# Gate and branch projections with 512 moving columns, a reordered beginning and a new weave in a hybrid decoder block

## The chip, the core and the metric

The kernel runs on one core of a Trainium2 chip. The metric is the device time of one execution in microseconds, lower is better; the time before is the median of three runs, 1659.07 us (1658.06 to 1659.58). TensorE (PE) multiplies, VectorE (DVE), ScalarE (ACT) and GpSimd (POOL) do the elementwise work, and SyncE (SP) issues most of the loads. PE takes a stationary operand of up to 128x128 (a weight load, PEld) and streams the columns of a moving operand past it into PSUM.

## What is computed

One layer (DEPTH is 1) of a decoder trunk over 256 tokens and 2048 channels in float32. Cut to what matters:

```python
mod = silu(c) @ w_ada + b_ada            # six vectors of 2048: sh1 sc1 g1 sh2 sc2 g2
h = rms_norm(x, mix_norm_pre) * (1 + sc1) + sh1
a_q, a_f, a_i, a_g, b_q, b_k, b_v, c_a, c_g = split(h @ w_in)
ya = hgrn2_mixer(a_q, a_f, a_i, a_g, ...)      # gated linear recurrence, 8 heads
yb = dilated_attention_mixer(b_q, b_k, b_v, rel_bias)
yc = conv_module(c_a, c_g, ...)                # 31-tap depthwise convolution, layer norm, swish
gates = sigmoid(h @ w_gate + b_gate)           # three gates of 2048 columns
merged = g0 * (ya @ w_a_out) + g1 * (yb @ w_b_out) + g2 * (yc @ w_c_out)
x = x + g1 * rms_norm(merged @ w_o, mix_norm_post)
h = rms_norm(x, mlp_norm_pre) * (1 + sc2) + sh2
x = x + g2 * rms_norm(square(relu(h @ w_up)) @ w_down, mlp_norm_post)
```

## The kernel before

All products of activations and weights are made in three passes of a reduced float type (fp32r). A weight tile of 128x1024 float32 (512 KB) is loaded into one of six `raw` buffers; ACT casts it into `hi` (line 126), DVE subtracts to get `lo` (line 127), six buffers each; PE then adds hi x hi, hi x lo and lo x hi. The work is a list of some 540 such **jobs**, run in order by `run`: it issues loads up to five jobs ahead and splits up to four jobs ahead, then emits the matmuls of job i, and then `work(budget)` lets generators emit a little side work: `chain` holds attention, the recurrence (`hgrn_prep`, `hgrn_levels`, `hgrn_out`) and small row builders, `filler` holds the convolution (`conv_gen`, 31 taps on DVE, line 452) and its layer norm. A scheduler then fixes the order on every engine, so each engine's queue is in order.

There are two ways to multiply. `mm_a` (lines 242 to 254) keeps 128 output channels on the PSUM partitions: the weight tile is stationary and the 256 tokens move, 24 matmuls of 256 columns in a job. `mm_b` (lines 256 to 266) keeps 128 tokens on the partitions: the activations are stationary and 512 weight columns move, 12 matmuls of 512 columns in a job.

```python
nc.tensor.matmul(o, h[:, i, w], x, start=f and b0, stop=False, skip_group_check=True)   # mm_a
nc.tensor.matmul(o, ah[i][:, tk], h[:, i, :], start=f, stop=False)                      # mm_b
```

The order of the jobs is: eight chunks of `wada0` (the modulation of the first 256 channels, made on PE by `ada_pe_jobs`); the 13 units of the input projection in four strips of the contraction (`start_job`, ten units by `mm_a`, three by `mm_b`); 20 `v_job`s (`mm_b`); 96 `gate_job`s and 32 `proj_job`s (`mm_a`); 32 `o_job`s (`mm_b`); up-projection; down-projection. Between them stand 184 `ada` jobs, which load 512 KB and make a weighted sum over it on DVE (line 297). `weave` spreads the last 128 of these (g1 and m2 before, g2 in the up-projection) over the main jobs by weights; before, the first 32 gate jobs (W0) have none.

A gate is finished by four ACT sigmoids of 256 columns with the bias as a per-partition scalar (line 840). A branch is finished by a product (line 900) and a sum (line 904) on DVE, the third branch also by a hi/lo split (lines 908, 909). Between the last `o_job` and the up-projection, per half of the tokens, stand a norm (`post_o`, `norm_x2`, `make_h2`) and the splits of the first up-projection tiles; four of these lo parts are made on POOL (`UPOOL`).

Of the kernel before, what the change touches and what calls it, by code (L numbers as in the profile page):

```python
# [56 lines left out]
def hybrid_block(ctx: ExitStack, tc: tile.TileContext, a, out, dbg=None):  # L57
# [216 lines left out]
    nc.vector.tensor_mul(cact, cact, V("c"))  # L274
    cbc = []

    def bcast_cols(ps, cols, n):

        for j in range(n):
            nc.tensor.matmul(ps[:, j * P:(j + 1) * P], cols[:, j:j + 1].to_broadcast([P, P]), ident, start=True, stop=True)  # L280

    def make_cbc():
        for q in range(2):
            cbc.append(s4([P, 1024]))
            ps = ps_unit().rearrange("p a b -> p (a b)")
            bcast_cols(ps, cact[:, 8 * q:8 * q + 8], 8)
            nc.scalar.copy(cbc[q], ps)
# [19 lines left out]
    def ada_pe_jobs(finish):  # L307

        st = {}

        def fn(raw, ch):
            if ch == 0:
                st["ps"] = bank()
            for i in range(2):
# [2 lines left out]
                nc.tensor.matmul(st["ps"][32 * g:32 * g + 32, :], cact[:, kt:kt + 1].to_broadcast([P, 32]), raw[:, i, :],
                                 start=kt < 4, stop=kt >= 12, skip_group_check=True)
            if ch == 3:
                make_cbc()  # L320
            if ch == 7:
                acc = s2([P, 512])
                nc.scalar.mul(acc, st["ps"], 1.0 / 32)
                ps = bank()
# [971 lines left out]
```

## Time and profile before

| | |
|---|---|
| median of three runs | 1659.07 us (1658.06 to 1659.58) |
| the profiled execution, its own time | 1659.91 us |
| its span, first to last instruction | 1658.1 us |
| PE busy | 1622.5 us (98% of the span) |
| DVE busy | 1201.3 us (72%) |
| ACT busy | 735.4 us (44%) |
| POOL busy | 47.2 us (3%) |
| DMA moved | 403.21 MB, mean 243 GB/s |

Busy time of PE is modelled: matmuls overlap, so the mean duration of one (284 ns for 256 columns) is more than the distance between two. The rate is read from how many matmuls stand in a window that PE fills. For the other engines the distance of two starts is a little less than a duration.

### The profile page before, as it was taken

What the parts mean: (1) busy time and instruction counts of PE and PEld (TensorE: products, weight loads), DVE (VectorE), ACT (ScalarE), POOL (GpSimd) and SP (SyncE); (2) the same over time, 40 slices, a digit from 0 to 9 for tenths busy, and PEclk for the clock granted to TensorE, in tenths of its full rate; (3) what the DMA queues carried; (4) which work ended last, traced back from release to release, by engine and by line L of the source; (5) the groups of instructions that cost most, each with busy time, mean ns of one, the idle gap of its engine ahead of it and who ended that gap; (6) DMA issues with size and microseconds to landing.
All of it is one profiled execution on the core that took longest, in us unless ns stands there. A gap on an engine that the chain in (4) does not pass through costs nothing.

```text
span 1658.1 us, 25901 instructions
## 1 busy us (share of the span) xinstructions
PE 1622.5 (98%) x10198; PEld 1453.8 (88%) x10198; DVE 1201.3 (72%) x1625; ACT 735.4 (44%) x899; POOL 47.2 (3%) x74
## 2 busy tenths in 40 slices
PE   5999999999999999999999899999999999999997
PEld 3899999978999999999988788888888888888886
DVE  6799989868798998887897766666566845444444
ACT  3644444354443454434444554444434644333333
POOL 1000002000000000000000300000000000000000
PEclk9999999999999999999999999999999999999999
DMA  8999997645353899899988467777777676666662
GB/s 300 324 328 336 325 334 252 180 144 166 98 158 95 281 320 369 333 350 328 315 323 305 157 228 243 235 243 244 241 249 245 208 222 206 193 191 197 193 192 77
DMA packets 112106, 403.21 MB, mean 243 GB/s; under 512 B 13124, under 2 KB 13552, under 8 KB 111984
## 3 DMA queue, kind: packets, MB, share of 16 engines
q1 hardware_dynamic: 107280, 388.24, 69.5%
q0 software_dynamic: 4416, 13.18, 2.7%
q8 instruction: 80, 1.31, 0.3%
q14 instruction: 42, 0.34, 0.1%
q10 hardware_dynamic: 288, 0.13, 0.0%
HBM read 397.28 MB, written 6.59 MB: 244 GB/s over the span
## 4 chain that ended last, share of the span: by engine, by line
PE 93%; DVE 3%; ACT 2%; DMA 1%; issue 1%; POOL 0%; DVEq 0%; SPq 0%; ACTq 0%; POOLq 0%
PE g L1093 14%; PE g L254 11%; PE g L252 11%; PE g L253 11%; PE g L1095 7%; PE g L1170 5%; PE g L1171 5%; PE g L1172 5%; PE g L266 4%; PE g L265 4%; PE g L264 4%; PE m L1170 2%; PE m L1171 2%; PE m L1172 2%; PE m L566 2%; DVE lo L127 1%
## 5 line engine op out<-in xcount | busy, mean ns | idle before, releaser
L126 ACT CAST hi<-raw 128x1024 fp32r<-128x1024 f32 x538 | 563.9, 1052 | 787.2 <-PE g L1093 190.0
L127 DVE TENSOR_TENSOR lo<-raw,hi 128x1024 fp32r<-128x1024 f32 x534 | 646.4, 1220 | 256.6 <-ACT hi L126 255.0
L254 PE MATMUL g<-s,lo 128*128 128x256 f32 x1600 | 455.3, 285 | 1.2 <-DVE lo L127 1.2
L252 PE MATMUL g<-s,hi 128*128 128x256 f32 x1600 | 454.9, 284 | 0.0
L253 PE MATMUL g<-s,hi 128*128 128x256 f32 x1600 | 454.1, 284 | 0.0
L1093 PE MATMUL g<-s,hi 128*128 128x512 f32 x960 | 336.5, 397 | 0.0
L254 PEld LDWEIGHTS g<-s,lo 128*128 128x128 f32 x1600 | 307.3, 192 | 2.8 <-DVE lo L127 2.1
L252 PEld LDWEIGHTS g<-s,hi 128*128 128x128 f32 x1600 | 307.4, 192 | 1.6 <-issue 1.5
L253 PEld LDWEIGHTS g<-s,hi 128*128 128x128 f32 x1600 | 307.4, 192 | 0.4 <-issue 0.3
L297 DVE SCALAR_TENSOR_TENSOR raw<-raw,s 128x1024 f32<-128x1024 f32 x184 | 223.9, 1218 | 112.9 <-DMA raw<-wada 112.9
L1095 PE MATMUL g<-s,lo 128*128 128x256 f32 x960 | 268.0, 279 | 0.0
L1093 PEld LDWEIGHTS g<-s,hi 128*128 128x128 f32 x960 | 180.4, 188 | 43.9 <-issue 0.9
L1095 PEld LDWEIGHTS g<-s,lo 128*128 128x128 f32 x960 | 181.0, 188 | 0.0
L1172 PE MATMUL g<-hi,s 128*128 128x512 f32 x384 | 149.6, 389 | 0.0
L1170 PE MATMUL g<-hi,s 128*128 128x512 f32 x384 | 149.5, 389 | 0.0
L1171 PE MATMUL g<-lo,s 128*128 128x512 f32 x384 | 149.5, 389 | 0.0
L266 PE MATMUL g<-hi,s 128*128 128x512 f32 (+1 forms) x344 | 132.7, 386 | 2.9 <-DVE s L971 2.3
L264 PE MATMUL g<-hi,s 128*128 128x512 f32 (+1 forms) x344 | 132.2, 384 | 0.0
L265 PE MATMUL g<-lo,s 128*128 128x512 f32 (+1 forms) x344 | 131.8, 383 | 0.3 <-DVE lo L127 0.3
L1172 PEld LDWEIGHTS g<-hi,s 128*128 128x128 f32 x384 | 72.1, 188 | 15.0
L1170 PEld LDWEIGHTS g<-hi,s 128*128 128x128 f32 x384 | 72.1, 188 | 15.0
L1171 PEld LDWEIGHTS g<-lo,s 128*128 128x128 f32 x384 | 72.1, 188 | 14.8
(223 smaller groups left out, 1369.7 us busy)
## 6 DMA issues: line engine op xcount, KB each, us to landing
raw<-wada SPq DMA_DIRECT2D x192, 512.0 KB, 5.2
raw<-wu SPq DMA_DIRECT2D x128, 512.0 KB, 4.6
raw<-wd SPq DMA_DIRECT2D x128, 512.0 KB, 4.3
raw<-wg SPq DMA_DIRECT2D x96, 512.0 KB, 4.8
raw<-w SPq DMA_DIRECT2D x80, 512.0 KB, 5.2
raw<-wv SPq DMA_DIRECT2D x44, 512.0 KB, 3.9
raw<-wp SPq DMA_DIRECT2D x32, 512.0 KB, 5.8
raw<-wo SPq DMA_DIRECT2D x32, 512.0 KB, 5.2
```

The costliest lines, as they stand in the source:

```text
L126: nc.scalar.copy(h, raw)
L127: (eng or nc.vector).tensor_sub(l, raw, h.bitcast(F32))
L252: nc.tensor.matmul(o, h[:, i, w], x, start=f and b0, stop=False, skip_group_check=True)
L253: nc.tensor.matmul(o, h[:, i, w], y, start=False, stop=False, skip_group_check=True)
L254: nc.tensor.matmul(o, l[:, i, w], x, start=False, stop=e and b1, skip_group_check=True)
L266: nc.tensor.matmul(o, al[i][:, tk], h[:, i, :], start=False, stop=e)
L297: nc.vector.scalar_tensor_tensor(raw, raw, 1.0, cbc[q % 2], op0=ALU.mult, op1=ALU.mult, accum_out=st["p"][:, q:q + 1])
L1093: nc.tensor.matmul(ps[:, j, :], h[:, i, w], xy.rearrange("p a b -> p (a b)"), start=f, stop=False, skip_group_check=True)
L1095: nc.tensor.matmul(ps[:, j, 0:S], l[:, i, w], xy[:, 0, :], start=False, stop=e, skip_group_check=True)
L1170: nc.tensor.matmul(o, uh[:, kt % 4, tk], h[:, 0, w], start=kt == 0, stop=False)
L1171: nc.tensor.matmul(o, uh[:, kt % 4, tk], l[:, 0, w], start=False, stop=False)
L1172: nc.tensor.matmul(o, ul[:, kt % 4, tk], h[:, 0, w], start=False, stop=kt == 63)
```

## The change

It has six parts. (1) `gate_job` and `proj_job` use `mm_b`. The bias of a gate is now a row: POOL loads 512 columns of it into all partitions, DVE adds it out of PSUM, and one ACT sigmoid follows. The merged sum has tokens on partitions, so `merge_gen` turns it by 8 PE transposes for each n, with the hi/lo split in two halves. (2) The beginning is one function `begin`: `wada0` goes to eight buffers of its own, the token sums use adds instead of reductions, and `issue_after` ties fix the order on PE, ACT and DVE. (3) `ADA_AT` lets the first ada job come after three start jobs. (4) W0 goes from 32 to 8, and the weights of the weave change; 40 of the m2 jobs come before the g1 jobs. (5) BLS, the budget of the last input strip, goes from 0.4 to 0.8. (6) `UPOOL` is empty.

```diff
-BLS = 0.4
+BLS = 0.8
+ADA_AT = 3.0
-W0 = 32
-WG = 1.25
-WG2 = 1.25
+W0 = 8
+WG = 0.75
-WO = 1.2
+WO = 0.9
...
-            nc.vector.tensor_reduce(rd, sq.rearrange("p k s -> p s k"), axis=AX.X, op=ALU.add)
-            if q:
-                nc.vector.tensor_add(rd, rd, tot)
+            nc.vector.tensor_add(sq[:, 0:2, :], sq[:, 0:2, :], sq[:, 2:4, :])
+            if tot is not None:
+                nc.vector.tensor_add(sq[:, 0:2, :], sq[:, 0:2, :], tot[:, 0:2, :])
...
+        for ch in range(8):
+            t = s4([P, 2, 512])
+            nc.sync.dma_start(t, a["wada0"][ch].rearrange("p (a b) -> p a b", a=2))
+            raws.append(t)
...
     def gate_job(b, n, ch):
...
-            mm_a(pst["gt"], h, l, 2, [h_hi(k) for k in kts], [h_lo(k) for k in kts], ch == 0, ch == 7)
+            mm_b(pst["gt"], h, l, 2, [h_hi(k) for k in kts], [h_lo(k) for k in kts], ch == 0, ch == 7)
             if ch == 7:
-                gates[b, n] = s4([P, 4, S])
-                for j in range(4):
-                    c = b * 16 + n * 4 + j
-                    g = nc.scalar.activation(gates[b, n][:, j, :], pst["gt"][:, j // 2, (j % 2) * S:(j % 2 + 1) * S],
-                                             AF.Sigmoid, bias=V("bg")[:, c:c + 1])
+                g = gates[b, n] = s4([P, 2, 512])
+                nc.vector.tensor_add(g, pst["gt"], pst["gb"][:, None, :].to_broadcast([P, 2, 512]))
+                e = nc.scalar.activation(g, g, AF.Sigmoid)
...
+    def merge_gen(n):
...
+        for q in range(2):
+            ps = bank()
+            for j in range(2):
+                for t in range(2):
+                    nc.tensor.transpose(ps[:, j * S + t * P:j * S + (t + 1) * P],
+                                        merged[n][:, t, (2 * q + j) * P:(2 * q + j + 1) * P], ident)
+            psv = ps.rearrange("p (a b) -> p a b", a=2)
+            k = slice(2 * q, 2 * q + 2)
+            nc.scalar.copy(mh[:, k, :], psv)
+            nc.vector.tensor_sub(ml[:, k, :], psv, mh[:, k, :].bitcast(F32))
+            yield 0.6
...
-            mm_a(pst["pj"], h, l, 2, [t[:, 0, 0, :], t[:, 0, 1, :]], [t[:, 1, 0, :], t[:, 1, 1, :]], first, last)
+            mm_b(pst["pj"], h, l, 2, [t[:, 0, 0, :], t[:, 0, 1, :]], [t[:, 1, 0, :], t[:, 1, 1, :]], first, last)
...
-    UPOOL = (4, 5, 6, 7)
+    UPOOL = ()
...
-    jobs += weave([(gj[W0:72], WG), (pj[:8], WP), (gj[72:], WG2), (pj[8:], WP), (oj[:-10], WO)], g1_jobs + m2_jobs)
+    jobs += weave([(gj[W0:72], WG), (pj[:8], WP), (gj[72:], WG), (pj[8:], WP), (oj[:-10], WO)],
+                  m2_jobs[:40] + g1_jobs + m2_jobs[40:])
```

The order of the instructions that follows from it is shown at three places. **PE at the very beginning.** L317 before and L326 after is the modulation of the first channels from `wada0` (`raw` before, `s` after), L280 and L284 are broadcasts of `cact` and of the token norm `xr`, L363 and L384 the token sums. Before:

```order
L317 MATMUL m_166<-raw_154,cact 32x512
L363 MATMUL g_101<-ones,s_13_118 128x1 x2
L317 MATMUL m_166<-raw_154,cact 32x512
L317 MATMUL m_166<-raw_156,cact 32x512 x2
L280 MATMUL g_182<-ident,cact 128x128 x2
L317 MATMUL m_166<-raw_158,cact 32x512 x2
L280 MATMUL g_182<-ident,cact 128x128 x2
L280 MATMUL g_101<-ident,xr_123 128x128 x2
L317 MATMUL m_166<-raw_160,cact 32x512 x2
L280 MATMUL g_182<-ident,cact 128x128 x4
L280 MATMUL g_193<-ident,cact 128x128 x8
L317 MATMUL m_166<-raw_162,cact 32x512 x2
```

And after:

```order
L284 MATMUL g_118<-ident,cact 128x128 x8
L284 MATMUL g_127<-ident,cact 128x128 x8
L326 MATMUL m_117<-s_5_101,cact 32x512 x2
L326 MATMUL m_117<-s_6_103,cact 32x512 x2
L384 MATMUL g_136<-ones,s_20_148 128x1 x4
L326 MATMUL m_117<-s_7_105,cact 32x512 x2
L326 MATMUL m_117<-s_8_107,cact 32x512 x2
L326 MATMUL m_117<-s_9_109,cact 32x512 x2
L284 MATMUL g_136<-ident,xr_164 128x128 x2
L326 MATMUL m_117<-s_10_111,cact 32x512 x2
```

The 16 broadcasts of `cact` now stand ahead of everything, and the loads they used to separate are no longer in the `raw` ring.

**DVE in the first woven gate jobs.** The `hgrn_levels` of the first four heads make seven levels; in each, PE multiplies, DVE copies under a mask (COPY_PREDICATED) and makes two products. L127 and L128 are the lo parts of gate jobs, L452 and L488 convolution taps, L878 the new gate bias. Before, levels three and four:

```order
L569 COPY_PREDICATED s_657_4195<-masks,m_4401 128x128x4
L577 TENSOR_TENSOR s_647_4122<-s_647_4122,s_666_4273 128x128x4
L578 TENSOR_TENSOR s_648_4123<-s_648_4123,s_666_4273 128x128x4
L583 TENSOR_TENSOR s_666_4273<-s_666_4273 128x16
L452 SCALAR_TENSOR_TENSOR s_698_4581<-s_693_4537,vec,s_698_4581 128x256 x2
L127 TENSOR_TENSOR lo_4622<-raw_4584,hi_4621 128x1024
L569 COPY_PREDICATED s_657_4195<-masks,m_4446 128x64x8
L577 TENSOR_TENSOR s_647_4122<-s_647_4122,s_666_4273 128x64x8
L578 TENSOR_TENSOR s_648_4123<-s_648_4123,s_666_4273 128x64x8
L452 SCALAR_TENSOR_TENSOR s_698_4581<-s_693_4537,vec,s_698_4581 128x256 x2
L127 TENSOR_TENSOR lo_4671<-raw_4619,hi_4670 128x1024
```

And after, levels five and six:

```order
L878 TENSOR_TENSOR s_698_4549<-g_4343,s_673_4344 128x1024
L488 SCALAR_TENSOR_TENSOR s_687_4450<-s_683_4426,vec,s_687_4450 128x256
L605 COPY_PREDICATED s_653_4197<-masks,m_4471 128x32x16
L613 TENSOR_TENSOR s_643_4124<-s_643_4124,s_662_4275 128x32x16
L614 TENSOR_TENSOR s_644_4125<-s_644_4125,s_662_4275 128x32x16
L488 SCALAR_TENSOR_TENSOR s_687_4450<-s_683_4426,vec,s_687_4450 128x256 x3
L605 COPY_PREDICATED s_653_4197<-masks,m_4500 128x16x32
L613 TENSOR_TENSOR s_643_4124<-s_643_4124,s_662_4275 128x16x32
L614 TENSOR_TENSOR s_644_4125<-s_644_4125,s_662_4275 128x16x32
L488 SCALAR_TENSOR_TENSOR s_687_4450<-s_683_4426,vec,s_687_4450 128x256 x2
L128 TENSOR_TENSOR lo_4618<-raw_4611,hi_4617 128x1024
```

Before, a lo part stood behind nearly every level; after, 33 rows stand between two lo parts here (the last 10 of them are shown).

**DVE between the output and the up-projection**, behind the scale of the first token half (`diag`). L962 and L1015 make h2, L971 and L1024 its lo part. Before, the lo parts of four more tiles are on POOL:

```order
L947 TENSOR_SCALAR diag_151<-ident,r_150 128x128
L127 TENSOR_TENSOR lo_9815<-raw_9680,hi_9814 128x1024
L127 TENSOR_TENSOR lo_9864<-raw_9686,hi_9863 128x1024
L962 TENSOR_SCALAR s_1430_9803<-m_9798,mod_86 128x128
L962 TENSOR_SCALAR s_1436_9823<-m_9818,mod_86 128x128
```

And after:

```order
L1000 TENSOR_SCALAR diag_223<-ident,r_222 128x128
L128 TENSOR_TENSOR lo_8325<-raw_8190,hi_8324 128x1024
L128 TENSOR_TENSOR lo_8374<-raw_8196,hi_8373 128x1024
L1015 TENSOR_SCALAR s_1446_8313<-m_8308,mod_86 128x128
L128 TENSOR_TENSOR lo_8406<-raw_8198,hi_8405 128x1024
L1015 TENSOR_SCALAR s_1446_8313<-m_8308,mod_86 128x128
L1015 TENSOR_SCALAR s_1452_8333<-m_8328,mod_86 128x128
L1024 TENSOR_TENSOR s_1447_8318<-s_1446_8313,s_1447_8318 128x2x128
L128 TENSOR_TENSOR lo_8412<-raw_8409,hi_8411 128x1024
```

Six lo parts now stand on DVE up to the second `diag`, where two did.

## Rows read from the trace of the kernel before

**Rows 1.** The page, part 1 and the chain that ended last.

```profile
PE 1622.5 (98%) x10198; PEld 1453.8 (88%) x10198; DVE 1201.3 (72%) x1625; ACT 735.4 (44%) x899; POOL 47.2 (3%) x74
...
PE 93%; DVE 3%; ACT 2%; DMA 1%; issue 1%; POOL 0%; DVEq 0%; SPq 0%; ACTq 0%; POOLq 0%
```

**Rows 2.** Windows: a stage of gate jobs and a stage of `mm_b` jobs.

```profile
core 0: us, PE busy (x) PEld busy (x) DVE busy (x) ACT busy (x) POOL busy (x), PEclk, DMA share, GB/s
...
700.00:750.00 50.00, 50.00 (x419) 50.00 (x418) 41.71 (x59) 21.42 (x26) 0.00 (x0) 1.00 0.96 349
850.00:900.00 50.00, 50.00 (x222) 41.45 (x221) 40.41 (x54) 22.08 (x28) 0.00 (x0) 1.00 0.94 351
```

**Rows 3.** Timeline of the beginning: start us, us, engine, line, operation.

```profile
3.07 16.66 SPq L112 DMA_DIRECT2D raw<-wada  x8
...
10.26 1.06 ACT L356 ACTIVATE s<-s 128x1024 f32<-128x1024 f32 x1 [0.23 <-DMA s<-xT]
...
17.09 0.16 DVE L215 TENSOR_SCALAR rv<-g 128x2 f32<-128x2 f32 x1 [1.10 <-PE g L363]
...
19.27 0.16 DVE L222 SCALAR_TENSOR_TENSOR xr<-rt,ry 128x2 f32<-128x2 f32 x1
...
27.10 1.92 PE L317 MATMUL m<-raw,cact 128*32 128x512 f32 x16
...
33.03 0.58 PE L252 MATMUL m<-s,hi 128*128 128x256 f32 x1 [2.21 <-ACT hi L126]
```

**Rows 4.** Window of gate jobs 9 to 36, columns as in rows 2.

```profile
451.40:564.30 112.90, 111.34 (x942) 110.63 (x941) 103.31 (x191) 49.78 (x94) 0.00 (x0) 1.00 0.50 158
```

**Rows 5.** Groups by line: busy us, mean ns, idle before, releaser.

```profile
L900 DVE TENSOR_TENSOR s<-g,s 128x1024 f32<-128x1024 f32 x12 | 14.7, 1221 | 2.5 <-PE g L254 2.4
...
L721 PE MATMUL m<-ident,s 128*128 128x128 f32 x36 | 6.1, 279 | 0.0
```

**Rows 6.** The chain in order of time: 16 matmuls of 128 columns in a row.

```profile
949.73 1.80 PE m L954 x16
```

**Rows 7.** Windows of the beginning, columns as in rows 2.

```profile
10.00:15.00 5.00, 1.88 (x2) 0.18 (x2) 5.00 (x4) 1.09 (x2) 0.00 (x0) 1.00 1.03 419
15.00:20.00 5.00, 3.96 (x16) 2.06 (x16) 2.92 (x15) 0.00 (x0) 3.09 (x7) 1.00 0.57 193
```

**Rows 8.** Waits from 34 to 250 us: us in total, times, longest.

```profile
ACT hi L126 <- DMA raw<-w: 49.9, 33, 3.4
```

**Rows 9.** Timeline of DVE: two lo parts in a row.

```profile
907.09 1.22 DVE L127 TENSOR_TENSOR lo<-raw,hi 128x1024 fp32r<-128x1024 f32 x1
908.22 1.22 DVE L127 TENSOR_TENSOR s<-raw,s 128x1024 fp32r<-128x1024 f32 x1
```

**Rows 10.** Groups by line in the window of rows 4, columns as in rows 5.

```profile
L127 DVE TENSOR_TENSOR lo<-raw,hi 128x1024 fp32r<-128x1024 f32 x29 | 35.3, 1217 | 1.2 <-ACT hi L126 1.2
L452 DVE SCALAR_TENSOR_TENSOR s<-s,vec,s 128x256 f32<-128x256 f32 x60 | 26.5, 477 | 0.0
L569 DVE COPY_PREDICATED s<-masks,m 128x512 f32<-128x512 uint8 x11 | 9.2, 837 | 8.2 <-PE m L566 8.2
L297 DVE SCALAR_TENSOR_TENSOR raw<-raw,s 128x1024 f32<-128x1024 f32 x7 | 8.5, 1213 | 0.0
L578 DVE TENSOR_TENSOR s<-s,s 128x512 f32<-128x512 f32 x12 | 8.2, 682 | 0.0
```

**Rows 11.** Timeline of POOL between output and up-projection.

```profile
925.76 7.70 POOL L127 TENSOR_TENSOR lo<-raw,hi 128x1024 fp32r<-128x1024 f32 x3 [106.15 <-ACT hi L126]
```

**Rows 12.** Timeline of DVE in the same place.

```profile
923.47 0.29 DVE L947 TENSOR_SCALAR diag<-ident,r 128x128 f32<-128x128 f32 x1
...
928.28 0.41 DVE L971 TENSOR_TENSOR s<-s,s 128x256 fp32r<-128x256 f32 x1
...
928.94 4.81 DVE L971 TENSOR_TENSOR s<-s,s 128x256 fp32r<-128x256 f32 x2
...
943.41 0.29 DVE L947 TENSOR_SCALAR diag<-ident,r 128x128 f32<-128x128 f32 x1
```

More of the change, by code (lines that the diff above doesn't have):

```diff
@@ L127, in split @@
             (eng or nc.vector).tensor_sub(l, raw, h.bitcast(F32))
+        if gate2:
+            gate[:] = gate2
         return h, l
@@ L274, in hybrid_block @@
     nc.vector.tensor_mul(cact, cact, V("c"))
+    h0 = []
     cbc = []
@@ L279, in bcast_cols @@
         for j in range(n):
[L280 removed]
+            m = nc.tensor.matmul(ps[:, j * P:(j + 1) * P], cols[:, j:j + 1].to_broadcast([P, P]), ident, start=True, stop=True)
+        return m.ins
     def make_cbc():
+        pss = []
         for q in range(2):
[L284 to L287, printed above, removed]
+            pss.append(ps_unit().rearrange("p a b -> p (a b)"))
+            bcast_cols(pss[q], cact[:, 8 * q:8 * q + 8], 8)
+        return pss
     def ada_jobs(ct0, n, finish, budget=0.0):
@@ L316, in fn, with finish @@
                 g = kt % 4
[L317 to L324, printed above, removed]
-                for j in range(4):
-                    nc.tensor.matmul(ps[:, j:j + 1], acc[:, j * P:(j + 1) * P], ones[:, 0:1], start=True, stop=True)
-                t = small([P, 4], "adat", bufs=3)
-                nc.vector.tensor_copy(t.rearrange("p (k s) -> p s k", s=2), ps[:, 0:4].rearrange("p (s k) -> p s k", s=2))
-                finish(t)
-        return [Job(a["wada0"][ch], [P, 2, 512], lambda r, ch=ch: fn(r, ch), ada=True, budget=0.0) for ch in range(8)]
+                m = nc.tensor.matmul(ps[32 * g:32 * g + 32, :], cact[:, kt:kt + 1].to_broadcast([P, 32]), raws[ch][:, i, :],
+                                     start=kt < 4, stop=kt >= 12, skip_group_check=True)
+            return m.ins
+        def finish():
+            acc = s2([P, 512])
+            c = nc.scalar.mul(acc, ps, 1.0 / 32)
+            gate[:] = [c.ins]
+            pt = bank()
+            for j in range(4):
+                nc.tensor.matmul(pt[:, j:j + 1], acc[:, j * P:(j + 1) * P], ones[:, 0:1], start=True, stop=True)
+            t = small([P, 4], "adat", bufs=3)
+            nc.vector.tensor_copy(t.rearrange("p (k s) -> p s k", s=2), pt[:, 0:4].rearrange("p (s k) -> p s k", s=2))
+            return t
+        return tile_of, finish
     def mod_cols(t, kt, dst, b, nw):
@@ L345, in hybrid_block, with begin @@
     hT = []
-    def load_x():
+    def begin():
         for q in range(4):
@@ L404, in fn @@
                 bias_load()
+            gate.clear()
+            gate2.clear()
             if ch == 0 and (u > 0 or s == 0):
@@ L781, in hybrid_block @@
     nc.scalar.dma_start(ident, a["ident"])
-    load_x()
-    jobs = ada_pe_jobs(lambda t: make_h(t, 0))
+    begin()
+    jobs = []
     sj, due = [], {}
@@ L792, in hybrid_block @@
     pos = []
-    at, j0 = 0.0, 0
+    at, j0 = ADA_AT, 0
     while j0 < 7:
@@ L886, in act_of @@
         return ycT[ki - 5]
+    def merge_gen(n):
+        for _ in range(MERGE_WAIT):
+            yield 0.0
+        mh, ml = s4([P, 4, S], F32R), s4([P, 4, S], F32R)
+        mhl[n] = (mh, ml)
+        for q in range(2):
+            ps = bank()
+            for j in range(2):
+                for t in range(2):
+                    nc.tensor.transpose(ps[:, j * S + t * P:j * S + (t + 1) * P],
[5 more added lines that the diff above has]
+            yield 0.6
+    MERGE_WAIT = 4
     def proj_job(n, ki):
```

77 lines of the change are left out of this document (48 added, 29 removed).

## The prediction

> **What bounds the kernel now.** I read the page first: PE is busy for 98% of the span and the chain that ended last lies on PE for 93% [rows 1]. So a microsecond less of PE work counts in full, as long as PE is fed. Busy time does not tell PE's rate, since its ends are modelled, so next I took windows that PE fills without a gap. In a gate stage 419 matmuls stand in 50 us, one per 0.1193 us; these are `mm_a`, 256 columns. In a stage of `mm_b`, 512 columns, 222 stand in 50 us, one per 0.2252 us, both at the full granted clock [rows 2]. Third, the timeline of the beginning: the first job's matmul starts only at 33.03 us [rows 3]. Fourth, the stretch in which the recurrence and the convolution run beside the gate jobs: there DVE is busy for 103.3 of 112.9 us [rows 4], so it is the place where PE can lose its food. I marked it by the order on PE: from the first matmul of gate job 9 to that of gate job 37.
>
> The sum is made against the profiled execution, 1659.9 us, 0.8 above the median of the three runs; its span is 1658.1 and 1.8 lie around it.
>
> **Wider moving operand.** A job goes from 24 matmuls at 0.1193, 2.863 us, to 12 at 0.2252, 2.702 us: 0.16 less. 96 gate and 32 branch jobs make 128 x 0.16 = 20.6 us; I take **-20**, bounds -19 and -21. The Trainium skill speaks against this term ("TensorE: Matmul & The Clock Gate", Back-to-back issue gap): the distance of isolated matmuls grows nearly in step with the columns, 262 cycles for 256 and 518 for 512. By it, as an estimate, a job would save 0.03 us and the whole term would be 4. The trace shows a wide matmul at 1.89 times a narrow one, not 1.98; the measurement decides.
>
> **Turning the merged sum.** 4 x 8 transposes of 128 columns are new on PE. The nearest rows: 36 transposes took 6.1 us with their ends, 0.17 each [rows 5], and 16 narrow matmuls in a row 0.1125 each [rows 6]. That bounds it by 3.6 and 5.4; I take **+4**, nearer the row without ends, since the transposes stand in a stream. The DVE product and sum stay 1.2 us each [rows 5]; the split only changes its shape. The product's reader on PE, the seventh and eighth output job, comes some 16 us later (six jobs of 2.7): hidden by those, at 2 us a job if that cover were gone.
>
> **Gate finish.** Four ACT sigmoids become a DVE sum out of PSUM, like line 900, 1.22 us [rows 5], and one ACT sigmoid. Three PSUM units rotate, so PE has two gates, some 40 us, before it needs the unit again: nothing on PE. On DVE it is 12 x 1.14 us, counted below where DVE is short. POOL issues 12 small loads; before, it was idle most of the run [rows 1], and a bias row is asked for eight jobs ahead of its use, 22 us: nothing.
>
> **The beginning.** Before, eight loads of `wada0` were issued over 16.7 us, because the six-buffer ring held the last ones back [rows 3], and DMA fell from 419 to 193 GB/s behind 15 us [rows 7]. With eight buffers of their own, the loads (6.3 MB with the tokens) stream at about 400 GB/s and have landed near 19 us. The other chain: squares end at 11.3 [rows 3]; two adds of 128x512 at 0.68 (like line 578 [rows 10]) give 12.7, where reductions went on to 16 before; token sums 1.1; the small root, 17.09 to 19.43, 2.3; a broadcast and its place behind three chunks, as an estimate, 2: 18 us. Three products on DVE, 128x1024 at 1.14 like a lo part [rows 9], make 21.6. From the last chunk's matmuls, which end at 29.02, to the first job matmul at 33.03 passed 4.0 [rows 3]; the cast of the first tile, 1 us of it, now stands ahead. So 3 more: 25 for 33, **-8**. Bounds -10 and -2: the loads bound the other end, since in the first input strip the casts wait for loads 33 times, 49.9 us in all [rows 8]. I take -8 because all eight loads of `wada0` and the first weight tiles are now queued without a break from the start, where the rate fell to 193 GB/s before [rows 7]. ADA_AT only shifts the ada loads inside that strip; BLS gives one convolution step per job for 0.4 and for 0.8 alike, because a step costs 0.8: both nothing.
>
> **The woven gate jobs 9 to 36.** Here W0 acts: ada jobs, which before began with gate job 33, now begin at job 9. Count of the DVE order between the lo parts of gate jobs 9 and 37, at distances of starts (a lo part 1.14 [rows 9]; taps and others their mean less the same 0.08 [rows 10]): before, 28 lo 31.9, 60 taps 23.8, 2 ada 2.3, recurrence and small work 49: 107. After: the same, with 13 ada more (14.9), four gate sums (4.6) and 8 of recurrence and attention that used to come earlier: **134.6**. PE's own work there is 28 x 2.702 + 300 narrow side matmuls at 0.1125 = 109.5, against 28 x 2.863 + 270 x 0.1125 = 110.5 before (942 matmuls less 28 x 24 [rows 4]); the 30 more are the recurrence's that used to come earlier. So the even spread that the change speaks of is not in the order: DVE gets 25 us more than PE has. What is paid is less: with six hi/lo buffers DVE can stand five jobs ahead, 5 x 2.7 and the side work between, 19.6, less one cast and one lo part, 2.3: 17 us. 134.6 - 109.5 - 17 leaves 8. DVE also waits for PE's level products, 8.2 us in this stretch before [rows 10]; in-order queues on both sides keep part of it, I take half: 12 us of PE waiting. Before, PE lost 112.9 - 110.5 = 2.4 [rows 4]. Net **+10**, bounds +2 and +31 (no lead, all waits). Behind job 37 eight jobs have 17 to 20 us of DVE and 21.6 of PE, so the lead comes back and costs nothing more. The ada jobs moved out of later stages were hidden there: nothing back.
>
> **No lo parts on POOL.** POOL's three took 7.70 us, and beside them two DVE subtractions took 4.81 us where one takes 0.41 [rows 11, 12]. Without them DVE has four lo parts more, 4.6 us, and loses some 4 to 6 of stretched time. From first to second `diag` 19.9 us before [rows 12]; the new order's rows add up to about 18.7. **-1**, bounds -3 and +3. The Trainium skill ("SBUF — State Buffer", Who interferes with whom) says that a DVE instruction with two SBUF inputs and a reading GpSimd instruction block each other outright; the 4.81 agrees, and by it alone the term would be -4.
>
> **Sum:** -20 + 4 - 8 + 10 - 1 = -15 against 1659.9: 1645, or 1644 on the median's scale.
>
> **Rivals.** (A) DVE becomes the bound in jobs 9 to 36 in full: the level products alternate between PE and DVE, so PE is blocked on them in order and its lead of split tiles buys nothing. For it: 33 rows of DVE work now stand between two lo parts. Against it: before, DVE was busy 91% there and PE still lost only 2.3. Price +31 in place of +10: 1665, **slower**. It turns slower at a price of about +28. (B) The lead covers the stretch, and DVE hardly waits since it is always behind: +2 to +3, with a beginning at -9: 1636. For it: side matmuls give DVE time. (C) The first strip is fed by loads just in time [rows 8], and the earlier start only moves the wait: -2 in place of -8, 1650. (D) The wider operand does not do what it says: 512 columns beside real gate weights cost twice 256. Then the term is 0 to -4, the rest -15 + 20 = +5 to +1: 1661 to 1664. The skill's rule named above would give this. Against it: the same `mm_b` runs at 0.2252 with other weights [rows 2].
>
> **How the numbers follow.** Forecast 0.62, A 0.08, B 0.15, C 0.12, D 0.03. A measurement here can tell 0.2%, 3.3 us. Faster: most of the forecast, all of B, most of C, 0.84. Slower: A, D's upper part and the forecast's far end, 0.10. Same 0.06. The range takes in B, C and the forecast with its bounds: 1634 to 1656; outside lie A, D and a rest of the forecast, under 2 in 10.
>
> **What would show it.** In the profile after: windows of the woven gate stage with about 222 matmuls in 50 us; the first job matmul at 23 to 27 us; PE waits on lo parts or recurrence products of some 10 us between gate jobs 9 and 36, with DVE above 95% there; 17 to 21 us from `diag` to `diag`. The prediction is wrong if PE in a filled gate window stays near 0.24 us a matmul, if the first strip idles for loads, or if the stretch costs over 25 us.

## The result and the profile after

The changed kernel takes 1667.88 us, the median of four runs (1665.70 to 1670.03), against 1658.57 before: ratio 1.0057, 95% interval 1.0040 to 1.0075. It is 0.6% slower, where 1644 was forecast. The profiled execution has a span of 1668.3 us, 10.2 more than before.

Part 1 of the page and the chain that ended last, answering to [rows 1]: PE has 8698 instructions for 10198 and the same busy time, and only 85% of the chain for 93%.

```profile
PE 1622.0 (97%) x8698; PEld 1387.3 (83%) x8698; DVE 1213.0 (73%) x1645; ACT 728.4 (44%) x867; POOL 42.9 (3%) x82
...
PE 85%; DVE 6%; DMA 5%; issue 2%; ACT 2%; SPq 0%; DVEq 0%; ACTq 0%
```

To see where, I took the first matmul of each job on PE in both traces. Jobs count from the first of the input projection; gate job 1 is job 124.

| stretch | before, us | after | difference | by the prediction |
|---|---|---|---|---|
| to the first job matmul | 33.0 | 26.5 | -6.6 | -8 with the next row |
| first 24 jobs | 75.2 | 73.2 | -2.0 | |
| last job of the input projection, 20 `v_job`s (103 to 123) | 80.2 | 77.5 | -2.8 | 0 |
| gate jobs 1 to 8 | 34.9 | 32.3 | -2.6 | -1.3 |
| gate jobs 9 to 36 | 112.9 | 133.2 | **+20.3** | +5.5 (+10 and 28 x -0.16) |
| gate jobs 37 to 52 | 52.9 | 56.8 | **+3.9** | -2.6 |
| gate jobs 53 to 72, 8 branch jobs | 81.6 | 76.7 | -4.9 | -4.5 |
| 24 gate and 24 branch jobs | 138.2 | 134.9 | -3.3 | -4.7 |
| first 8 output jobs | 21.8 | 32.5 | **+10.7** | +1 |
| output jobs 25 to 32, 18 of the up-projection | 87.9 | 84.6 | -3.4 | -1 |
| the next 140 jobs (110 up, 30 down) | 391.7 | 393.3 | +1.6 | 0 |

The stretches between are the same, and what is behind differs by 0.8 us. What was to be gained came. Windows of the changed kernel, columns as in [rows 2]: a gate stage now has 222 matmuls in 50 us, the rate of `mm_b`; the second row answers to [rows 4].

```profile
630.00:680.00 50.00, 50.00 (x222) 41.42 (x221) 43.02 (x57) 23.91 (x23) 0.00 (x0) 1.00 0.96 370
437.50:570.70 133.20, 123.00 (x638) 103.80 (x636) 117.11 (x223) 42.33 (x77) 1.08 (x2) 0.91 0.48 149
```

In the second, PE is idle for 10.2 us and its granted clock is 0.91 on the mean, where it was 1.00. The timeline of the beginning answers to [rows 3]: all eight loads are issued by 12.5, the squares end later than before, at 13.2, the root starts at 16.8, and the first job matmul at 26.5.

```profile
3.07 9.38 SPq L318 DMA_DIRECT2D s<-wada  x8
...
12.13 1.06 ACT L370 ACTIVATE s<-s 128x1024 f32<-128x1024 f32 x1 [0.81 <-DMA s<-xT]
...
16.80 0.16 DVE L218 TENSOR_SCALAR rv<-g 128x2 f32<-128x2 f32 x1 [1.56 <-PE g L384]
...
26.48 0.80 PE L255 MATMUL m<-s,hi 128*128 128x256 f32 x2 [1.28 <-ACT s L410]
```

From `diag` to `diag` it is 17.3 us for 19.9 [rows 12], on the timeline of DVE:

```profile
936.14 0.28 DVE L1000 TENSOR_SCALAR diag<-ident,r 128x128 f32<-128x128 f32 x1
...
953.41 0.29 DVE L1000 TENSOR_SCALAR diag<-ident,r 128x128 f32<-128x128 f32 x1
```

**Gate jobs 9 to 36.** The groups of PE in the window 437.5 to 570.7 (last columns: busy, mean ns, idle before) show that PE waits less for lo parts (0.8) than for the recurrence: the level products, L602, wait for DVE.

```profile
L268 PE MATMUL g<-lo,s 128*128 128x512 f32 x112 | 46.7, 417 | 0.9 <-DVE lo L128 0.8
...
L602 PE MATMUL m<-s,s 128*128 128x64 f32 x208 | 30.3, 308 | 9.1 <-DVE s L614 6.5 <-DVE adat L307 2.3 <-DVE s L619 0.2
```

The timelines of PE, then DVE, follow. Between two levels PE's queue has a level product at its head and stands for 2.08 us; DVE waits 1.93 us for PE in its turn, then has three operations to make before PE may go on. No split tile is left behind that product: the first matmul of gate job 12 ran at 453.78, but its lo part is made only at 461.06, 26 us behind the end of the one before it (of gate job 11, begun at 433.83). At the other waits before L602 it is the same: gate jobs 23 and 27 get their lo parts at 513.06 and 534.34, behind the waits.

```profile
451.53 1.89 PE L602 MATMUL m<-s,s 128*128 128x64 f32 x16
...
455.50 2.93 PE L602 MATMUL m<-s,s 128*128 128x64 f32 x16 [1.32 <-DVE s L614]
460.50 1.73 PE L602 MATMUL m<-s,s 128*128 128x64 f32 x7 [2.08 <-DVE s L614]
...
573.20 0.50 PE L268 MATMUL g<-lo,s 128*128 128x512 f32 x1 [2.13 <-DVE lo L128]
```

```profile
418.52 1.23 DVE L128 TENSOR_TENSOR lo<-raw,hi 128x1024 fp32r<-128x1024 f32 x1 [1.71 <-ACT hi L127]
...
433.83 1.22 DVE L128 TENSOR_TENSOR lo<-raw,hi 128x1024 fp32r<-128x1024 f32 x1
...
458.46 0.72 DVE L605 COPY_PREDICATED s<-masks,m 128x512 f32<-128x512 uint8 x1 [1.93 <-PE m L602]
459.08 0.68 DVE L613 TENSOR_TENSOR s<-s,s 128x512 f32<-128x512 f32 x1
459.67 0.68 DVE L614 TENSOR_TENSOR s<-s,s 128x512 f32<-128x512 f32 x1
...
461.06 1.22 DVE L128 TENSOR_TENSOR lo<-raw,hi 128x1024 fp32r<-128x1024 f32 x1
```

So the lead was used up. The lo part of gate job 9 is ready at 419.75, 17.8 us before its job; that of gate job 37, made from 571.93, is what PE waits for at 573.20. From the one to the other DVE took 153.4 us where PE took 133.2, and the 20.2 between them are the lead and the 2.5 by which the last lo part came after the start of its job. Windows from the lo part of gate job 9 to that of 37, before and after (third: DVE busy), and the group before which DVE was idle most, after:

```profile
434.65:551.07 116.42, 115.88 (x981) 114.99 (x980) 106.49 (x195) 49.80 (x91) 0.00 (x0) 1.00 0.41 126
```

```profile
418.52:571.93 153.41, 141.86 (x739) 119.05 (x738) 133.81 (x251) 54.74 (x95) 1.08 (x2) 0.92 0.48 151
```

```profile
L605 DVE COPY_PREDICATED s<-masks,m 128x512 f32<-128x512 uint8 x14 | 12.4, 887 | 12.9 <-PE m L602 12.2 <-issue 0.6
```

DVE was idle for 19.6 us of it, where it had been for 9.9 before.

Windows of 2 us around the two waits (the third number from the right is the granted clock): it falls from 1.00 to 0.50, the level of 1.2 GHz, among the level products that follow the idle time of 1.32 us, and before that of 2.08. The 16 products take 2.93 us, where 16 at full clock took 1.89.

```profile
452.00:454.00 2.00, 2.00 (x16) 1.70 (x15) 1.09 (x3) 1.06 (x1) 0.00 (x0) 1.00 0.00 0
454.00:456.00 2.00, 0.68 (x6) 0.53 (x5) 2.00 (x5) 0.00 (x0) 0.00 (x0) 1.00 0.00 0
456.00:458.00 2.00, 2.00 (x13) 2.00 (x12) 0.54 (x2) 0.00 (x0) 0.00 (x0) 0.57 0.00 0
458.00:460.00 2.00, 0.43 (x2) 0.24 (x2) 1.54 (x3) 0.00 (x0) 0.00 (x0) 0.50 0.00 0
```

I summed by what each matmul's distance to the next exceeds that of its width at full clock (0.227, 0.120, 0.1125 us). These **losses** come to 23.7 us in gate jobs 9 to 36, against 3.8 before: 10.2 are idle time, and some 10 are the lower clock behind it: the mean clock of 0.91 is 12 us of clock lost in 133.2, some 2 of them while PE stood idle. In gate jobs 37 to 52 they are 10.0 against 3.3. So the woven stretch loses 26.6 us more up to job 52, while the matmuls themselves need what was predicted.

**The first output jobs.** The timeline of PE: the eight transposes of the last merged sum stand in front of the second output job and wait 7.05 us; the matmuls behind them are 0.43 us apart, not 0.227. Then that of DVE: the sum, L961, comes at 849.07, and before it DVE waited 5.26 and 1.74 us for `wada` loads.

```profile
842.91 0.39 PE L269 MATMUL g<-hi,s 128*128 128x512 f32 x1
850.34 1.97 PE L936 MATMUL m<-ident,s 128*128 128x128 f32 x8 [7.05 <-DVE s L961]
...
852.54 0.63 PE L268 MATMUL g<-lo,s 128*128 128x512 f32 x1
852.96 0.63 PE L269 MATMUL g<-hi,s 128*128 128x512 f32 x1
```

```profile
827.11 1.23 DVE L303 SCALAR_TENSOR_TENSOR raw<-raw,s 128x1024 f32<-128x1024 f32 x1 [5.26 <-DMA raw<-wada]
...
832.41 1.23 DVE L303 SCALAR_TENSOR_TENSOR raw<-raw,s 128x1024 f32<-128x1024 f32 x1 [1.74 <-DMA raw<-wada]
...
849.07 1.22 DVE L961 TENSOR_TENSOR s<-s,s 128x1024 f32<-128x1024 f32 x1
```

Why the load was late stands on POOL's timeline: the last row of g1 (L900) waited 38.08 us at the head of POOL's queue for DVE's copy of it, and the loads of x behind it, 512 KB each, then left together. The list of DMA issues from 800 to 845 us (count, KB, median us to landing) and the chain follow: x took 12.2 us in the median (6.1 before), and the `wada` load issued at 816.19 took 10.89 where 4.8 is usual.

```profile
810.26 0.52 POOL L900 DMA_DIRECT2D np_scratch<-s  x1 [38.08 <-DVE s L897]
814.49 0.56 POOL L901 DMA_DIRECT2D s<-np_scratch  x1 [3.71 <-DMA np_scratch<-s]
815.04 2.14 POOL L1042 DMA_DIRECT2D s<-x  x3
```

```profile
raw<-wada SPq DMA_DIRECT2D x9, 512.0 KB, 4.8
...
s<-x POOLq DMA_DIRECT2D x4, 512.0 KB, 12.2
```

```profile
816.19 10.89 DMA raw<-wada
```

### The profile page after: what moved, and what is told of

Read it like the earlier page. It is cut to its first block, busy times and chain, and to the rows that moved or that the text cites. A ratio compares the mean times of both kernels' runs of the same rounds, so it can differ in the third digit from the quotient of the medians.

```text
span 1668.3 us, 22852 instructions
## 1 busy us (share of the span) xinstructions
PE 1622.0 (97%) x8698; PEld 1387.3 (83%) x8698; DVE 1213.0 (73%) x1645; ACT 728.4 (44%) x867; POOL 42.9 (3%) x82
## 4 chain that ended last, share of the span: by engine, by line
PE 85%; DVE 6%; DMA 5%; issue 2%; ACT 2%; SPq 0%; DVEq 0%; ACTq 0%
PE g L1146 13%; PE g L267 9%; PE g L268 9%; PE g L269 9%; PE g L1148 7%; PE g L1226 5%; PE g L1225 5%; PE g L1224 5%; PE g L255 4%; PE g L257 4%; PE g L256 4%; DVE lo L128 2%; DMA raw<-wg 2%; PE m L1226 2%; PE m L1225 2%; PE m L1224 2%
## 5 line engine op out<-in xcount | busy, mean ns | idle before, releaser
L127 ACT CAST hi<-raw 128x1024 fp32r<-128x1024 f32 x538 | 564.1, 1052 | 806.4 <-PE g L1146 186.3
L128 DVE TENSOR_TENSOR lo<-raw,hi 128x1024 fp32r<-128x1024 f32 x538 | 653.6, 1221 | 277.6 <-ACT hi L127 275.7
L268 PE MATMUL g<-lo,s 128*128 128x512 f32 (+1 forms) x856 | 335.1, 391 | 4.0 <-DVE lo L128 3.9
L267 PE MATMUL g<-hi,s 128*128 128x512 f32 (+1 forms) x856 | 335.2, 392 | 0.0
L269 PE MATMUL g<-hi,s 128*128 128x512 f32 (+1 forms) x856 | 334.0, 390 | 0.0
L1148 PE MATMUL g<-s,lo 128*128 128x256 f32 x960 | 269.5, 281 | 0.0
L1146 PEld LDWEIGHTS g<-s,hi 128*128 128x128 f32 x960 | 180.1, 188 | 44.1 <-issue 0.9
L268 PEld LDWEIGHTS g<-lo,s 128*128 128x128 f32 x856 | 162.6, 190 | 39.2 <-DVE lo L128 6.7
L267 PEld LDWEIGHTS g<-hi,s 128*128 128x128 f32 x856 | 162.6, 190 | 33.5 <-issue 1.2
L269 PEld LDWEIGHTS g<-hi,s 128*128 128x128 f32 x856 | 162.3, 190 | 33.1 <-issue 1.3
L1148 PEld LDWEIGHTS g<-s,lo 128*128 128x128 f32 x960 | 181.4, 189 | 0.0
L255 PE MATMUL g<-s,hi 128*128 128x256 f32 x576 | 163.4, 284 | 0.6 <-ACT hi L127 0.6
L257 PE MATMUL g<-s,lo 128*128 128x256 f32 x576 | 163.1, 283 | 0.0
L256 PE MATMUL g<-s,hi 128*128 128x256 f32 x576 | 163.0, 283 | 0.0
L255 PEld LDWEIGHTS g<-s,hi 128*128 128x128 f32 x576 | 110.7, 192 | 1.6 <-ACT hi L127 0.9
L257 PEld LDWEIGHTS g<-s,lo 128*128 128x128 f32 x576 | 110.6, 192 | 0.6 <-issue 0.6
L256 PEld LDWEIGHTS g<-s,hi 128*128 128x128 f32 x576 | 110.7, 192 | 0.0
```

The lines of the kernel that those rows point to most:

```text
L127: nc.scalar.copy(h, raw)
L256: nc.tensor.matmul(o, h[:, i, w], y, start=False, stop=False, skip_group_check=True)
L257: nc.tensor.matmul(o, l[:, i, w], x, start=False, stop=e and b1, skip_group_check=True)
L268: nc.tensor.matmul(o, ah[i][:, tk], l[:, i, :], start=False, stop=False)
L269: nc.tensor.matmul(o, al[i][:, tk], h[:, i, :], start=False, stop=e)
L1146: nc.tensor.matmul(ps[:, j, :], h[:, i, w], xy.rearrange("p a b -> p (a b)"), start=f, stop=False, skip_group_check=True)
```

## The experiments

Each was timed beside the kernel before on the same chip; the ratio is to that. Five chips were used, on which the kernel before has medians of 1658.2 to 1659.5 us, so two experiments are compared to within about 1 us beside their own spread.

**e1: the weave of before in the changed kernel.**

```diff
-W0 = 8
-WG = 0.75
-WO = 0.9
+W0 = 32
+WG = 1.25
+WO = 1.2
...
-                  m2_jobs[:40] + g1_jobs + m2_jobs[40:])
+                  g1_jobs + m2_jobs)
```

> The changed kernel with the weave of before alone: 32 gate jobs without ada jobs, the old weights, g1 before m2. Theory (the ada jobs in gate jobs 9 to 36 make DVE the bound there): the stretch from gate job 9 to 37 falls from 133.2 us to 106-113, the next 16 jobs from 56.8 to about 50, and the whole to about 1644 (1637 if the 7.2 us wait of the turned sum at 843 us goes too). Rival (the wide gate jobs and their sums on DVE starve PE, whatever the weave): 1663 to 1669.

Measured 1651.58 us, ratio 0.9948 (0.9929 to 0.9968): 16.3 less than the changed kernel. Gate jobs 9 to 36 take 111.0 us, as the theory said. But the 44 jobs behind it (37 to 80 in the expectations; the last eight are branch jobs) take 141.8, where the changed kernel has 133.5: with more ada jobs here PE loses 17 us. The wait for the turned sum stays at 3 us. So the whole is above the forecast of 1644.

**e2: the wide jobs alone, in the kernel before.**

```diff
-            mm_a(pst["gt"], h, l, 2, [h_hi(k) for k in kts], [h_lo(k) for k in kts], ch == 0, ch == 7)
+            mm_b(pst["gt"], h, l, 2, [h_hi(k) for k in kts], [h_lo(k) for k in kts], ch == 0, ch == 7)
...
-            mm_a(pst["pj"], h, l, 2, [t[:, 0, 0, :], t[:, 0, 1, :]], [t[:, 1, 0, :], t[:, 1, 1, :]], first, last)
+            mm_b(pst["pj"], h, l, 2, [t[:, 0, 0, :], t[:, 0, 1, :]], [t[:, 1, 0, :], t[:, 1, 1, :]], first, last)
```

> The kernel before with the wide gate and branch jobs, the gate sum on DVE and the turning of the merged sum, and nothing else. Theory: 128 jobs of 12 matmuls at 0.225 us save 20 us, 32 transposes cost 4, and PE waits 0 to 7 us for a turned sum: 1643 to 1650. Rival (the wide operand hardly saves: 4 us in all): 1659 to 1666.

Measured 1663.42 us, ratio 1.0021 (1.0008 to 1.0034). The theory missed, and the rival's number came by another way: eight fed gate jobs do take 21.8 us for 23.0, but jobs 37 to 80 take 140.8 us for 134.5, and the first eight output jobs 28.0 for 21.8, with this row on PE's timeline:

```profile
841.02 1.97 PE L900 MATMUL m<-ident,s 128*128 128x128 f32 x8 [3.63 <-DVE s L925]
```

A PE that is faster by 6% is one that the same loads and a DVE with the gate sums on top (1.2 us each) no longer feed.

**e3: the new beginning alone, in the kernel before** (`begin` with its ties, and ADA_AT).

> The kernel before with the new beginning alone (and the ada loads after three start jobs). Theory (the 8.6 us gained by job 24 stay to the end, and nothing behind them is pushed): 1650, first job matmul at 26.5 us. Rival (what the beginning gains is waited for later, since the side work behind it is not ready earlier): 1655 to 1660 with the first matmul at 26.5 all the same.

Measured 1648.95 us, ratio 0.9935 (0.9920 to 0.9950). The theory holds: the whole gain of the beginning reaches the end.

**e4: less DVE time in the first 16 woven ada jobs of the changed kernel** (15/16 of each sum is left out).

```diff
-            raw = raw[:, 0, :]
+            raw = raw[:, 0, :w]
...
+ w=64 if i < 2 else 1024
```

> The changed kernel; the first 16 woven ada jobs, which stand in and around gate jobs 9 to 40, sum over 64 of their 1024 columns, so this leaves out 15/16 of those sums; their loads of 512 KB and their buffers stay. Theory (DVE time is what is short): 16 x 1.06 = 17 us less on DVE, the time falls by 13 to 20 us, to 1648-1655. Rival (the loads and the six-buffer ring are what is short, not DVE): it falls by under 4 us, 1664 to 1668.

Measured 1652.55 us, 15.3 less than the changed kernel. Gate jobs 9 to 36 take 121.7 us for 133.2, and the idle time before L602 is 3.9 us for 9.1. The theory holds: DVE's time is what is short, and the loads, which are all still there, are not.

**e5: half the loads of the 96 ada jobs, in e2.**

```diff
+                for c in range(2):
+                    nc.vector.scalar_tensor_tensor(raw[:, 0, 512:], raw[:, 0, 0:512], 1.0, cbc[q % 2][:, 512 * c:512 * c + 512],
```

> The kernel of e2 (wide jobs alone); the 96 ada jobs for g1 and m2 load 256 KB in place of 512 KB and sum the same half twice, so this leaves out the other half of their data; the time on DVE stays (two operations of 512 columns, 1.2 to 1.3 us). Theory (with the old weave the transfers bound the wide gate jobs from job 33 on, 1.00 DMA share at 381 GB/s): the stretch of gate jobs 37 to 80 falls from 140.8 us to 125-130, the whole from 1663 to 1649-1655. Rival (DVE is what is short there): 1660 to 1665.

Measured 1677.42 us, ratio 1.0117: a miss. Half the bytes made it slower. The two operations cost DVE more than one, so this run had two changes in it; e9 parts them. Most of what its profile lost against e2 lies further back, in the 24 gate and 24 branch jobs, 147.4 us for 135.4.

**e9: DVE's sums cut, all loads kept, in e1** (as e4, for all 96).

> The kernel of e1 (the change with the old weave); all 96 ada jobs for g1 and m2 sum over 64 of their 1024 columns (15/16 of these sums are left out), their loads of 512 KB stay. Theory (DVE is what the wide gate jobs lack from job 33 on, as the slower e5 with its longer sums on DVE suggests): gate jobs 37 to 80 fall from 141.8 us to 125-130, the wait for the last turned sum goes, the whole 1632 to 1641. Rival (the loads and the six-buffer ring are short, 1.00 DMA share at 381 to 387 GB/s): that stretch stays at 137-142 us, the whole 1645 to 1652.

Measured 1639.52 us, ratio 0.9886 (0.9869 to 0.9902), 12.1 less than e1. The windows of jobs 37 to 80 in e2, e5, e1 and e9, one fence each (third: DVE busy; last: DMA share, GB/s):

```profile
557.20:698.00 140.80, 132.48 (x567) 104.55 (x566) 127.26 (x185) 64.02 (x71) 7.48 (x14) 0.99 0.94 339
```

```profile
556.20:700.70 144.50, 134.46 (x566) 104.93 (x565) 131.44 (x273) 64.78 (x71) 7.47 (x14) 0.98 0.80 266
```

```profile
549.60:691.30 141.70, 133.26 (x569) 104.72 (x568) 125.82 (x184) 63.98 (x71) 7.47 (x14) 0.99 0.93 334
```

```profile
549.00:681.00 132.00, 130.11 (x566) 105.00 (x565) 86.90 (x180) 62.51 (x69) 7.47 (x14) 0.99 0.96 359
```

With fewer bytes and more DVE time the stretch is longer; with all bytes and less DVE time it is 9.7 us shorter. So DVE binds here too, for the most part: e9 is still 2 us over the 130 that I had set as the top, and the casts there still wait for loads, 43.5 us in 27 times; whether that is what is left isn't shown.

**e6** set MERGE_WAIT to 8 in e1, and changed no instruction: its empty steps cost 0.0, so all pass at once.

> The kernel of e1 (the change with the old weave), the turning of a merged sum two jobs later (MERGE_WAIT 8 for 4). Theory (PE only stands at the head of its queue for a sum that DVE has not reached; four jobs, 11 us, are enough): the eight jobs behind the last branch job fall from 27.3 us to 22-23, the whole from 1651.6 to 1645-1648. Rival (the wait only moves to the output jobs that read the sum): 1650 to 1653.

Measured 1651.91 us: the same program as e1 again, 0.3 us from it. **e10** gives each step a cost, and the transposes then stand two jobs later.

```diff
         for _ in range(MERGE_WAIT):
-            yield 0.0
+            yield 1.4
...
-    MERGE_WAIT = 4
+    MERGE_WAIT = 8
```

> The kernel of e1 with the turning of a merged sum two jobs later; a cost of 1.4 at each of eight empty steps, where the 0.0 of e6 let all of them pass at once. Theory (PE stands at the head of its queue for a sum that DVE has not reached): the eight jobs behind the last branch job fall from 27.3 us to 22.5-23.5, the whole from 1651.7 to 1646-1648.5. Rival (the wait moves to the output jobs that read the sum): 1650 to 1653.

Measured 1650.87 us, ratio 0.9953 (0.9937 to 0.9968). The stretch did as the theory says, 22.7 us for 27.3; the whole did not. In the profiled execution jobs 63 to 80, where nothing was edited, lost 6 us more than in e1. One profile doesn't say whether that is chance.

**e7: ada jobs from gate job 25 on, in e6** (W0 24, WG 1.0, WO 1.0).

> The kernel of e6 with the ada jobs from gate job 25 on and flatter weights (W0 24, WG 1.0, WO 1.0): 0.85 ada jobs for each gate job, 1.36 MB... in 2.72 us less than 360 GB/s. Theory (gate jobs 9 to 24 need DVE for the recurrence, the later ones the transfers): 1638 to 1645, no stretch of gate jobs 37 to 96 over 2.75 us a job. Rival (DVE is short again in gate jobs 25 to 36): 1647 to 1655, with PE waiting for lo parts there.

Measured 1657.73 us: what the rival said, and above its range. Some eight ada jobs more before gate job 37 bring PE's losses in gate jobs 9 to 36 to 16 us, for 4 in e1, with PE waiting for lo parts (L268, 3.6 us of idle time). Beside the recurrence there is no room for even eight. (The 1.36 MB of the expectation is a slip: 1.85 tiles of 0.524 MB are 0.97 MB.)

**e8: BLS 0.8 alone, in the kernel before.**

> The kernel before with BLS 0.8 for 0.4 and nothing else. Theory (it fills the last input strip with convolution taps, so that less of them stands beside the recurrence, as the 2.7 us between jobs 103 and 124 of the changed kernel say, which the kernels e2 and e3 without it don't gain): 1655.5 to 1657. Rival (the prediction's: nothing): 1658.5 to 1660.

Measured 1656.74 us, ratio 0.9992 (0.9982 to 1.0001). The `v_job`s gain the 2.7 us; gate jobs 9 to 16 take 2.7 longer and the ten behind them 1.6 less, so 1.3 is left by gate job 37. In the whole it can't be told from none.

**e12: 16 of the m2 jobs between jobs 92 and 108, the rest from gate job 33 on, the turn delayed. e11: the same with narrow jobs.**

```diff
+    nj, early = 0, []
+    for j in jobs:
+        early.append(j)
+        nj += not j.ada
+        if not j.ada and 93 <= nj < 109:
+            early.append(m2_jobs.pop(0))
+    jobs = early
```

> The kernel of e10, with 16 of the m2 ada jobs moved in between jobs 92 and 108, where DVE is idle for a third and the transfers for half of the time, and the weave of the other 80 at the density that ran without waits in the changed kernel (0.69 for each gate job from 33 on). Theory (DVE is neither short beside the recurrence nor behind it): stalls of gate jobs 37 to 80 from 17 us to under 5, the whole 1633 to 1640. Rival (the early ada jobs delay the input projection's or the recurrence's work on DVE as much as they did in gate jobs 9 to 36): 1645 to 1655.

> As e12 but with the narrow gate and branch jobs of before (no turning, bias on ACT). Theory (a wide job that is fed saves 0.16 us): e12 plus 13 to 16 us, 1648 to 1653. Rival (even fed, the wide jobs save at most 5 us): within 5 us of e12.

e12 takes **1639.70 us**, ratio 0.9885 (0.9870 to 0.9900): it beats both kernels. Jobs 37 to 80 take 131.3 us, where e1 had 141.8, and gate jobs 9 to 36 take 111.1 us at full clock:

```profile
441.00:552.10 111.10, 109.73 (x618) 93.67 (x617) 102.15 (x188) 43.26 (x77) 0.54 (x1) 1.00 0.40 133
```

e11 takes 1665.46 us, 25.8 more and far above its forecast. About 16 of it is what the wide jobs were forecast to save. The narrow kernel also lost 9 us in its branch jobs to waits that e12 doesn't have, so the difference is not the wide jobs' alone. The best narrow kernel here is e3, with a ratio of 0.9935: against it e12, with a weave that feeds the wide jobs, gains 0.5% more, some 8 us.

**e13 and e14: the two causes taken away singly in the changed kernel.** e13 is the delayed turn of e10, e14 the 16 early jobs of e12 (W0 32).

> The changed kernel with the turning of a merged sum two jobs later and nothing else. Theory (the wait of 7.2 us and 2.5 us of half clock behind it are lost time): the eight jobs behind the last branch job fall from 32.5 us to 22.5-25, the whole from 1667.9 to 1657.5-1661. Rival (as in e10, other waits take its place): 1664 to 1668.

> The changed kernel with the 16 ada jobs of gate jobs 9 to 32 moved in between jobs 92 and 108, and nothing else. Theory (DVE time beside the recurrence is the price, 27 us of waits and half clock between gate jobs 9 and 52): those waits fall from 33.7 us to 8-10, some 3 us come back between jobs 103 and 124, the whole 1644 to 1649, and with e13's gain it reaches e12's 1639.7. Rival (the waits come from the order of DVE beside the recurrence and move with any weave): over 1655.

e14: 1646.30 us, 21.6 less than the changed kernel, as expected. e13: 1666.24, a miss. PE's timeline says what came in place of the wait: DVE has the sum still later, at 851.75, and the seventh output job waits for its lo part (L941).

```profile
853.10 1.07 PE L936 MATMUL m<-ident,s 128*128 128x128 f32 x8 [1.49 <-DVE s L961]
...
863.61 0.50 PE L269 MATMUL g<-hi,s 128*128 128x512 f32 x1 [2.70 <-DVE s L941]
```

**e15: lo parts on POOL again, in e12** (UPOOL 4 to 7).

> The kernel of e12 with four lo parts back on POOL (UPOOL 4 to 7). Theory (the empty UPOOL is a gain of 2.5 to 3.5 us, as the stretch from the last output jobs to the sixteenth up-projection job says, 87.2 to 87.9 us in five kernels with POOL and 84.6 to 85.1 in seven without): 1642 to 1643.5. Rival (what is gained there is lost to longer DVE work before): 1638.5 to 1640.5.

Measured 1639.72 us: no difference. The stretch is 2.1 us longer (87.2), and these subtractions on DVE take 4.80 us again:

```profile
909.20 4.80 DVE L1033 TENSOR_TENSOR s<-s,s 128x256 fp32r<-128x256 f32 x2
```

In the profiled executions the 140 jobs behind it took 391.7 us in e15 and 394.6 in e12, which happens to hide it (below). The term stays unsettled in the whole.

**e16: g1 ahead of m2 in e13. e17: m2 ahead of g1 in e12.**

> The kernel of e13 with the g1 ada jobs ahead of m2, as before the change. Theory (m2 ahead of g1 puts the last g1 row late on POOL's queue, the loads of x leave at once behind it, and DVE waits for an ada load that they delay): the x loads leave singly before 815 us, the eight jobs behind the last branch job fall from 29.8 us (e13) to 22.5-24, the whole from 1666.2 to 1656-1661. Rival (DVE's own work is too long there whatever the loads do): 1663 to 1668, with the same wait.

> The kernel of e12 with 24 more m2 ada jobs ahead of g1, as in the change. Theory (the same burst on POOL's queue comes back): three loads of x leave together near 792 us, the eight jobs behind the last branch job rise from 22.7 us to 28-31, the whole from 1639.7 to 1644-1648. Rival (the order does not matter once DVE is not behind): 1638.5 to 1641.5.

e16: 1652.40 us, 13.8 less than e13 and less than forecast. The loads of x leave singly, on POOL's timeline, and the first eight output jobs take 24.5 us for 29.8.

```profile
791.08 0.72 POOL L1042 DMA_DIRECT2D s<-x  x1 [30.76 <-DVE adat L307]
807.10 0.70 POOL L1042 DMA_DIRECT2D s<-x  x1 [15.30 <-DVE s L961]
815.06 0.72 POOL L1042 DMA_DIRECT2D s<-x  x1 [7.25 <-DVE s L961]
```

Gate jobs 9 to 52 also fell, by 7.7 us; why, no run separates. e17: 1642.18 us, the burst is back, and the output jobs take 26.5 us for 22.7. The direction is the theory's, the size half of it; in the whole the intervals of e17 (0.9882 to 0.9912) and e12 overlap.

```profile
791.35 0.52 POOL L909 DMA_DIRECT2D np_scratch<-s  x1 [35.35 <-DVE s L906]
...
794.78 2.14 POOL L1051 DMA_DIRECT2D s<-x  x3
```

## Why the prediction was wrong

- **Wider moving operand, -20, and transposes, +4: right as PE's work.** The rate is 222 in 50 us, and with the transposes a fed stretch gains what the sum says: in e12 24 gate and 24 branch jobs take 133.4 us for 138.2, -4.8, where 48 x -0.16 and 24 transposes at 0.1125 make -5.0. Rival D is out. What failed is the condition in the prediction's first lines, "as long as PE is fed": in e2, with the old weave, the wide jobs alone gain nothing (ratio 1.0021).
- **The beginning, -8: right.** -8.6 by job 24, and e3 keeps it to the end. Two errors offset each other: the first job matmul came 1.5 us later than forecast (the squares ended 1.9 later, the steps behind them took 13.3 us for 13.7), and the first strip then took 2.0 us less, which was not forecast. Rival C is out.
- **The woven gate jobs, +10: the failing step.** The count of DVE's work was right: 133.8 us busy between the two lo parts, where 134.6 was counted. The lead was about right too, 17.8 us for 17, and it was used up in full. Wrong was the term for DVE's own waits. The prediction took 4 us, half of the 8.2 of [rows 10]; DVE was idle for 19.6, of which 12.9 stand before the level copies, where it waits for PE. PE and DVE wait for each other in turn at the levels, and behind its own waits PE makes the products at half clock (2.93 us for 1.89), while DVE waits. The sign "DVE above 95% there" failed with it: 88%. PE's losses rose by 19.9 us in gate jobs 9 to 36, where +10 was forecast, and by 6.7 behind them, where "the lead comes back and costs nothing more": up to job 52 no lo part is more than 8.2 us ahead. Rival A, at 0.08, had this alternation, but with a lead that "buys nothing" and +31. That its 1665 lies near the measured 1668 is in part luck, since 9.8 us of that come from the output jobs. e4 shows that DVE's time is the price, e14 that 16 jobs elsewhere give 21.6 us back.
- **The clock was no term at all.** Before, the granted clock is 1.00 in [rows 4], so the rows gave no price; but [rows 3] had the first matmul at 0.58 us, after a wait. Of the 23.7 us lost in gate jobs 9 to 36 some 10 are slow matmuls behind a wait, as much as the waits themselves.
- **Turning the merged sum, "hidden by those": wrong.** I hid the product's reader behind six output jobs, but the transposes stand in PE's queue one job behind, and PE can't pass them: 9.8 us lost. The prediction also gave no term to the 40 m2 jobs that now come before g1; on POOL's queue the g1 row then stands late in front of the loads of x. With g1 first and the old weave (e1) the wait is 3 us; in the changed kernel the turn delayed alone gives 1.6 us, within the noise, and g1 first 13.8 more, of which 5.4 lie at this place and 7.7 in gate jobs 9 to 52, unexplained.
- **BLS, nothing: right in the whole, wrong in the reason.** It moves taps into the last strip; what the `v_job`s gain, gate jobs 9 to 16 give back (e8). ADA_AT was not tried alone.
- **No lo parts on POOL, -1:** the place gained 3.4 us, and six profiles with POOL have 87.2 to 87.9 us there, against 84.6 to 85.1 in thirteen without. Times of the whole don't confirm it (e15).
- **Gate finish, nothing:** PE waits for no gate's PSUM unit.

The losses of the woven stretch missed by 16.6 us and the turned sum by 9.8, 26.4 together. The median missed the forecast by 23.9, the profiled execution missed its sum by 25. What is left are smaller differences of either sign, the largest the POOL term, 2.4 better than taken.
